# Seventy-four weight blocks of an encoder layer whose high part comes by a rounding transfer and whose low part is finished by an adding one

## The chip, the cores and the metric

The kernel runs on one core of one Trainium2 chip, in a single launch. The metric is the device time of one execution in microseconds. Its median before the change is 818.35 us over three runs, which lie between 818.23 and 818.53 us.

In the text TensorE appears in profile rows as PE (its weight loads as PEld), VectorE as DVE, ScalarE as ACT, GpSimd as POOL, and SyncE, which only issues transfers here, as SP.

## The reference, cut to what matters

One layer of a bidirectional encoder on 512 rows of width 1024 in float32, with retention, a spatial gating unit and a gated MLP of width 2816 with a short convolution:

```python
h = rmsnorm(x, g_pre_mix)
proj = h @ w_in                                        # 1024 x 7168: q k v g u sv a_ret a_sgu
y_ret = (layernorm(retention(q, k, v)) * silu(g)) @ w_ret_o
y_sgu = (gelu(u) * spatial(layernorm(gelu(sv)))) @ w_sgu_o
merged = sigmoid(a_ret) * y_ret + sigmoid(a_sgu) * y_sgu
x = x + rmsnorm(merged @ w_out, g_post_mix)
h2 = rmsnorm(x, g_pre_ffn)
hid = conv3(h2 @ w_up) + conv_b                        # 1024 x 5632
a, b = split(hid, 2)
x = x + rmsnorm((gelu(a) * b) @ w_down, g_post_ffn)    # 2816 x 1024
```

Nearly all the work is in products with weights. Together the weights are 146 blocks of 128 partitions by 1024 float32 numbers, 512 KB each, and every block is used by all 512 rows.

## The kernel before, in words

**Products in two parts.** TensorE multiplies in a shorter float32 form (`F32R`). To keep accuracy, each operand is written as a high part (the number rounded to that form) and a low part (what the rounding left over, rounded in turn). A product is three matmuls added up in PSUM: high by high, high by low and low by high (`mm3`, L230 to L233; `t_group`, L543 to L545; `Pair.product`, L762; `products`, L1170; `add_whole`, L1186). For activations and weights alike the two parts come from `split` (L100): ScalarE copies the source into the high tile (L95), which rounds it, and VectorE subtracts that from the source into the low tile (L102).

**Weight units.** The 146 blocks of `wall` lie in HBM in the order in which they are used. Some are taken whole, others are first combined into sums, so that fewer products are needed (a Strassen-like scheme). A list of units, written out by hand at the start, says in which order they are prepared:

- `blk` is one whole block (`w_block`, L145). It takes two slots of the weight ring, one for the high and one for the low part.
- `B11`, `B21`, `T1`, `T2`, `T3`, `T4`, `B22` are half-size forms made from a pair of blocks (`w_form`, L167); T1 and T3 are sums made on VectorE, T2 and T4 on GpSimd from the gates on (L181, L184). Each takes one slot, which holds both parts.
- `q` and `t` are the down projection's quarter forms (`w_down`, L192). Each takes two slots.

The **weight ring** has nine slots (`slot`, L142; the tag `w4`). It is handed out in turn: a unit gets the slot that nine slots earlier belonged to another unit, and may be written only when TensorE's last matmul that reads the earlier content has ended. The unit is prepared ahead of its use: `w_get` (L217) walks the list, as far ahead as the ring has room.

In the kernel before, every block comes over SP's queue into a **raw tile** of its own, of which there are four. `w_block` starts that load as soon as a raw tile is free, and then has `split` write the two slots. So what has to happen between a slot coming free and TensorE reading it is one ScalarE copy and one VectorE subtraction; the raw block is there already.

**The stages**, in order of time: q and k (whole blocks 0 to 7, to about 190 us with the retention's own work beginning); V, SV and g (whole blocks 8 to 31, four to a `t_group`, to about 414 us with retention between); u (forms alone); the gates (blocks 40 to 71, eight `gated_pair`s of one form pair and two whole blocks each); the output projection (blocks 72 to 79, of which 74 to 79 are kept in resident tiles of another pool); the up projection (blocks 80 to 123), whose hidden tiles are paired into eight **couples** (`Pair.part1`, `f_block`, `part2`, `f_block` with `part3` in its middle) except for tiles 0 to 3, 20 and 21, which use whole blocks; the down projection (blocks 124 to 145, nine `q`/`t` pairs and two whole blocks in each half) and the final norm.

In a pair of gates and in a couple, the units are prepared in the order B11, B21, T1, T2, whole block, T3, T4, B22, whole block. TensorE uses them in nearly this order: four products with B11, B21, T1 and T2, a complete `f_block` with the first whole block, a product with T3, half an `f_block` with the second whole block, products with T4 and B22, and the other half.

**What sets the order.** Each engine carries out its instructions in the order in which they stand in its own list. A scheduling layer arranges them from the program's order; `behind()` (L284) holds whole blocks behind the first two. An engine that waits for a semaphore keeps everything behind it waiting; this goes for the queue on which GpSimd issues transfers too, since the issues stand among its ordinary instructions. Before the change GpSimd has some T2 and T4 sums, small sums of the gates and norms, and a few loads and stores of activations.

Of the kernel before, what the change touches and what calls it, by code (L numbers as in the profile page):

```python
# [12 lines left out]
AF = mybir.ActivationFunctionType  # L13
ALU = mybir.AluOpType
# [5 lines left out]
KD = D // P  # L20
# [12 lines left out]
DOWN0 = NW - NF  # L33
# [3 lines left out]
UP0 = DOWN0 - 2 * NF  # L37
EARLY = 4
# [9 lines left out]
def tile_block(ctx: ExitStack, tc, xT, x, wall, par, cs, wsp, bsp, gpost, gffn, out):  # L48
    nc = tc.nc
# [6 lines left out]
    def nm(s):  # L56
        uid[0] += 1
        return f"{s}_{uid[0]}"

    def blk(dt=F32, n="blk", shape=(P, S)):  # L60
        return sb.tile(list(shape), dt, tag="blk", bufs=NBLK, name=nm(n))
# [35 lines left out]
    def as32(t):  # L97
        return t.bitcast(F32)

    def split(hi, lo, src):  # L100
        copy(hi, src)
        nc.vector.tensor_sub(lo, src, as32(hi))  # L102
# [3 lines left out]
    RES1 = NW - 22 - 44  # L106
    RES0 = RES1 - RES_OUT
    FORMS = ("B11", "B21", "T1", "T2", "T3", "T4", "B22")
    units = []
    i = 0  # L110
    while i < NW:
# [7 lines left out]
        elif i == UP0 + 2 * COUPLES[0][0]:  # L119
# [3 lines left out]
            i = UP0 + 2 * COUPLES[-1][1] + 2  # L123
# [12 lines left out]
    def raw_tile():  # L136
        return sb.tile([P, 1024], F32, tag="raw", bufs=4, name=nm("raw"))


    AT_64, AT_192 = 16, 48  # L140

    def slot(n, at=0, w=1024):  # L142
        return sb.tile([P, 1088], F32R, tag="w4", bufs=9, name=nm(n))[:, at : at + w]

    def w_block(i):  # L145
        raw = raw01[i] if i < 2 else raw_tile()
        resident = RES0 <= i < RES1
        if i > 1:
            nc.sync.dma_start(raw, wall[i])
        if resident:  # L150
            hi, lo = [], []
            for c in range(2):
                h_, l_ = blk(F32R, "wh"), blk(F32R, "wl")
                split(h_, l_, raw[:, c * S : (c + 1) * S])
                hi.append(h_)
                lo.append(l_)
        else:
            at = AT_192 if i >= DOWN0 else AT_64 if UP0 <= i < UP0 + EARLY else 0
            hi, lo = slot("wh", at), slot("wl", at)
            if i < 2:  # L160
                first_blocks(i, hi, lo, raw)
            else:
                with behind():
                    split(hi, lo, raw)
        return hi, lo
# [45 lines left out]
    def w_unit(u):  # L211
        return w_block(u[1]) if u[0] == "blk" else (w_down if u[0] in "qt" else w_form)(*u)
# [71 lines left out]
    def behind():  # L284

        both = ExitStack()
        for ins in lasts:
            both.enter_context(tc.issue_after(ins))
        return both

    def first_blocks(i, hi, lo, raw):

        last = {}

        def w_high(f, eng=copy):
            return eng(hi[:, f], raw[:, f])

        def w_low(f):
            return nc.vector.tensor_sub(lo[:, f], raw[:, f], as32(hi[:, f]))

        a, b, c = PIECES
        steps = (
            (x_high, 0, x01[0], T0), (w_high, a, nc.vector.tensor_copy), (w_high, b), (w_low, a), (w_low, b),
            (x_low, 0, x01[0], T0), (x_high, 0, x01[0], T1), (x_low, 0, x01[0], T1), (w_high, c), (w_low, c),
        ) if i == 0 else (
            (x_high, 1, x01[1], slice(0, S)), (x_low, 1, x01[1]),
            (w_high, HALVES[0]), (w_low, HALVES[0]), (w_high, HALVES[1]), (w_low, HALVES[1]),
        )
        for f, *args in steps:
            last[f] = tc.keep_in_program_order(f(*args))  # L310
        lasts[:] = last[w_high].ins, last[w_low].ins
# [75 lines left out]
    for t in range(NT):  # L387
        for n in range(2):
# [3 lines left out]
                out=xt, in_=xt, func=AF.Square, accum_out=ss[:, 4 * n + t : 4 * n + t + 1]  # L392
# [20 lines left out]
    for c in range(19, 1, -2):  # L413
        v.scalar_tensor_tensor(
            out=lc, in0=lc, scalar=1.0 / c, in1=lb, op0=ALU.add, op1=ALU.mult
        )
    v.scalar_tensor_tensor(out=lc, in0=lc, scalar=1.0, in1=la, op0=ALU.add, op1=ALU.mult)
    with behind():
        v.tensor_scalar(out=lg, in0=lgt, scalar1=0.0, scalar2=None, op0=ALU.min)
    v.scalar_tensor_tensor(  # L420
        out=lg, in0=lc, scalar=-2.0, in1=lg, op0=ALU.mult, op1=ALU.add
# [707 lines left out]
    i = 0  # L1129
# [335 lines left out]
```

## Time and profile before

| what | before |
|---|---|
| median of three runs | 818.35 us (818.23 to 818.53) |
| span of the profiled execution | 817.4 us |
| PE busy | 809.1 us, 99% |
| DVE busy | 659.9 us, 81% |
| ACT busy | 441.3 us, 54% |
| POOL busy | 86.0 us, 11% |
| moved by SP's queue | 86.76 MB |
| moved by GpSimd's queue | 4.46 MB |

The profile is one execution recorded by the hardware profiler. Its rows give a group of equal instructions by line, engine, output and inputs, shapes and count, then the busy time, the mean length of one in ns, and the idle time of that engine just before them with what ended it. Matmuls are pipelined: the length of one row is longer than the distance to the next, so the pace is read from start to start. The view of windows gives, for a stretch of time, each engine's busy time, the granted TensorE clock (1.00 is full) and the share of the 16 transfer engines in use. The view of transfers gives the time from issue to landing. The chain of waits is followed back from the last instruction of the program.

### The profile page before, as it was taken

The numbers are of one execution on the slowest core, as the hardware profiler recorded it, in microseconds if no ns is written. First come the engines' busy times: TensorE is split into PE (matmuls) and PEld (weight loads), VectorE is DVE, ScalarE is ACT, GpSimd is POOL, SyncE is SP. The second block draws the span as 40 slices with busy tenths as digits, with TensorE's granted clock in tenths as the row PEclk, the third lists the DMA queues.
The fourth block names the chain that finished last, engine by engine and source line by source line (L and its number), as shares of the span: only waits on it lengthen the run. The fifth ranks groups of instructions, "written<-read, shape, count | busy, mean of one in ns | idle before, by whom it ended". The sixth has DMA issues, their size and how long they took to land. (4 is left out here: it accounts for less than half of the span.)

```text
span 817.4 us, 13292 instructions
## 1 busy us (share of the span) xinstructions
PE 809.1 (99%) x5163; PEld 730.4 (89%) x5163; DVE 659.9 (81%) x1115; ACT 441.3 (54%) x777; POOL 86.0 (11%) x93
## 2 busy tenths in 40 slices
PE   9999999999999999999999999999999999999996
PEld 7888888888999999999988898899999898999996
DVE  7479897877898777767765659989999989987877
ACT  6546445536675444444445577556666666544441
POOL 0010000110001111132210210110111200000001
PEclk9999999999999999999999999999999999999998
DMA  8733222221333332233349111333333341233244
GB/s 287 259 117 103 78 79 77 77 79 65 103 103 105 104 103 90 91 103 103 107 165 335 53 51 66 104 103 104 104 103 103 103 156 52 77 130 110 97 155 155
DMA packets 29647, 93.24 MB, mean 114 GB/s; under 512 B 3536, under 2 KB 4432, under 8 KB 29584
## 3 DMA queue, kind: packets, MB, share of 16 engines
q1 hardware_dynamic: 27360, 86.76, 31.5%
q0 software_dynamic: 1360, 4.46, 1.6%
q10 hardware_dynamic: 864, 1.18, 0.4%
q8 instruction: 40, 0.66, 0.3%
q14 instruction: 23, 0.19, 0.1%
HBM read 88.19 MB, written 4.19 MB: 113 GB/s over the span
## 5 line engine op out<-in xcount | busy, mean ns | idle before, releaser
L102 DVE TENSOR_TENSOR wl<-raw,wh 128x1024 fp32r<-128x1024 f32 (+1 forms) x92 | 108.5, 1187 | 42.5 <-PE ps L762 20.0
L95 ACT ACTIVATE wf<-raw 128x512 fp32r<-128x512 f32 x140 | 85.0, 626 | 99.3 <-PE ps L232 34.0
L102 DVE TENSOR_TENSOR wf<-raw,wf 128x512 fp32r<-128x512 f32 x140 | 106.5, 773 | 25.3 <-ACT wf L95 24.5
L762 PE MATMUL ps<-sh,wf 128*128 128x256 f32 x640 | 118.8, 277 | 0.2 <-ACT c L95 0.2
L95 ACT ACTIVATE wh<-raw 128x1024 fp32r<-128x1024 f32 (+2 forms) x96 | 93.3, 983 | 39.2 <-PE ps L545 15.8
L762 PEld LDWEIGHTS ps<-sh,wf 128*128 128x128 f32 x640 | 100.9, 188 | 1.0 <-ACT c L95 0.4
L232 PE MATMUL ps<-h2l,wh 128*128 128x512 f32 (+1 forms) x256 | 92.5, 363 | 0.0
L231 PE MATMUL ps<-h2h,wh 128*128 128x512 f32 (+1 forms) x256 | 92.4, 364 | 0.0
L233 PE MATMUL ps<-h2h,wl 128*128 128x512 f32 (+1 forms) x256 | 92.3, 361 | 0.0
L762 PE MATMUL ps<-sl,wf 128*128 128x256 f32 x320 | 88.5, 277 | 0.0
L543 PE MATMUL ps<-wh,xh 128*128 128x512 f32 x192 | 75.0, 391 | 0.0
L544 PE MATMUL ps<-wl,xh 128*128 128x512 f32 x192 | 74.8, 390 | 0.0
L545 PE MATMUL ps<-wh,xl 128*128 128x512 f32 x192 | 74.7, 389 | 0.0
L762 PEld LDWEIGHTS ps<-sl,wf 128*128 128x128 f32 x320 | 60.1, 188 | 0.6
L1170 PE MATMUL ps<-dl,fh 128*128 128x256 f32 x216 | 59.8, 277 | 0.0
L1170 PE MATMUL ps<-dh,fh 128*128 128x256 f32 x216 | 59.7, 277 | 0.0
L1170 PE MATMUL ps<-dh,fl 128*128 128x256 f32 x216 | 59.7, 277 | 0.0
L233 PEld LDWEIGHTS ps<-h2h,wl 128*128 128x128 f32 x256 | 48.0, 188 | 7.7
L231 PEld LDWEIGHTS ps<-h2h,wh 128*128 128x128 f32 x256 | 47.8, 188 | 7.2 <-ACT h2h L994 0.3
L232 PEld LDWEIGHTS ps<-h2l,wh 128*128 128x128 f32 x256 | 48.1, 188 | 6.6
L762 PE MATMUL ps<-xh,wf 128*128 128x256 f32 x288 | 53.9, 278 | 0.0
L95 ACT ACTIVATE dh<-raw 128x768 fp32r<-128x768 f32 (+1 forms) x36 | 33.6, 949 | 34.4 <-DVE raw L204 18.9
(314 smaller groups left out, 2037.4 us busy)
## 6 DMA issues: line engine op xcount, KB each, us to landing
raw<-wall SPq DMA_DIRECT2D x144, 512.0 KB, 3.6
x<-x SPq DMA_DIRECT2D x24, 256.0 KB, 6.2
x<-x POOLq DMA_DIRECT2D x8, 256.0 KB, 2.4
xT<-xT SPq DMA_DIRECT2D x7, 256.0 KB, 4.7
xT<-xT POOLq DMA_DIRECT2D x4, 256.0 KB, 3.3
out<-zg SPq DMA_DIRECT2D x4, 256.0 KB, 2.0
raw<-wall SPq DMA_DIRECT2D x3, 256.0 KB, 4.7
out<-zs ACTq DMA_DIRECT2D x3, 256.0 KB, 2.4
```

Of the source, the lines that this page charges most:

```text
L95: return nc.scalar.activation(out=o, in_=i, func=AF.Copy)
L102: nc.vector.tensor_sub(lo, src, as32(hi))
L231: nc.tensor.matmul(o, ah, bh, start=start, stop=False, skip_group_check=skip)
L232: nc.tensor.matmul(o, ah, bl, start=False, stop=False, skip_group_check=skip)
L233: nc.tensor.matmul(o, al, bh, start=False, stop=stop, skip_group_check=skip)
L543: nc.tensor.matmul(acc[t], xh[k][:, c], wh[:, f], start=k == 0, stop=False)
L544: nc.tensor.matmul(acc[t], xh[k][:, c], wl[:, f], start=False, stop=False)
L545: part_end[0] = nc.tensor.matmul(acc[t], xl[k][:, c], wh[:, f], start=False, stop=k == KD - 1)
L762: self.last = nc.tensor.matmul(o, w_[:, c], a_, start=first and k == n == 0, stop=k == 3 and n == 2, skip_group_check=True,)
L1170: nc.tensor.matmul(o, a_[:, c], w_[:, f], start=j == t == i == 0, stop=j == DP - 1 and i == 2 and n not in (M2, M3, M4), skip_group_check= ...
```

## The change

For every whole block from the ninth on (`i >= KD`, with `KD` = 8) that is not one of the six resident ones, the raw tile, the load over SP's queue and the `split` are left out. In their place a new helper `w_added` gives the block two slots and does three things:

1. a transfer issued by GpSimd brings the block from HBM straight into the high slot, and converts float32 into the short form on the way;
2. ScalarE writes the negative of the high part into the low slot (an activation with scale −1);
3. a second transfer issued by GpSimd reads the same block from HBM again and adds it onto what stands in the low slot, so that raw minus high is left there.

These are 74 blocks: 24 of V, SV and g, 16 of the gates, 2 of the output projection, 28 of the up projection and 4 of the down projection. VectorE loses 74 subtractions of 128 x 1024, SP loses 74 loads, GpSimd gains 148 transfers, ScalarE has 74 copies as before, with another source. The order of TensorE's matmuls stays as it was, but for 27 in the last rows. Forms, `q` and `t` units, the first eight blocks and the resident ones are made as before.

```diff
@@ -142,9 +142,19 @@
     def slot(n, at=0, w=1024):
         return sb.tile([P, 1088], F32R, tag="w4", bufs=9, name=nm(n))[:, at : at + w]
 
+    def w_added(i, at):
+
+        hi, lo = slot("ah", at), slot("al", at)
+        nc.gpsimd.dma_start(hi, wall[i])
+        nc.scalar.activation(out=lo, in_=as32(hi), func=AF.Copy, scale=-1.0)
+        nc.gpsimd.dma_start(lo, wall[i], accum_op=ALU.add)
+        return hi, lo
+
     def w_block(i):
+        resident = RES0 <= i < RES1
+        if i >= KD and not resident:
+            return w_added(i, AT_192 if i >= DOWN0 else AT_64 if UP0 <= i < UP0 + EARLY else 0)
         raw = raw01[i] if i < 2 else raw_tile()
-        resident = RES0 <= i < RES1
         if i > 1:
             nc.sync.dma_start(raw, wall[i])
         if resident:
```

Line numbers of the changed kernel are ten higher from `w_block` on (its matmuls of `mm3` are L241 to L243, for instance); the three new operations are L148, L149 and L150.

## The prediction

> **What bounds the kernel now.** I read the busy table and the slices first, then what PE waits for, then the queues.
>
> ```profile
> span 817.4 us, 13292 instructions
> PE 809.1 (99%) x5163; PEld 730.4 (89%) x5163; DVE 659.9 (81%) x1115; ACT 441.3 (54%) x777; POOL 86.0 (11%) x93
> PE   9999999999999999999999999999999999999996
> q1 hardware_dynamic: 27360, 86.76, 31.5%
> q0 software_dynamic: 1360, 4.46, 1.6%
> ```
> ```profile
> PE ps L324 <- PEq L1455: 0.8, 1, 0.8
> PE ps L762 <- ACT c L95: 0.2, 1, 0.2
> ```
>
> (Queues: packets, MB, share of the span; waits: us, times, longest.) The second fence is the whole list of PE's waits: 1.0 us. TensorE sets the time; everything else matters only where it becomes late for TensorE. The profiled execution, 817.4 us, stands 0.95 below the median of 818.35; I add that at the end. Differences under 0.2% (1.6 us) cannot be told from none here.
>
> So the question is not what the change frees but whether the new way of making a weight block fits between the moment its slot in the ring of nine comes free and the moment TensorE needs it. Today a raw block is loaded ahead into one of four other tiles, and after the slot is free only two operations remain:
>
> ```profile
> L102 DVE TENSOR_TENSOR wl<-raw,wh 128x1024 fp32r<-128x1024 f32 x80 | 101.0, 1263 | 40.9 <-PE ps L762 20.0 <-issue 7.0 <-ACT wh L95 5.8
> L95 ACT ACTIVATE wh<-raw 128x1024 fp32r<-128x1024 f32 x80 | 84.5, 1057 | 35.3 <-PE ps L545 15.8 <-DMA raw<-wall 10.9 <-PE ps L762 4.7
> ```
>
> That is 1.06 + 1.26 = 2.3 us. Afterwards the rounding transfer writes the slot itself, so it cannot start earlier than the slot is free; the chain becomes transfer, ScalarE's negative, adding transfer.
>
> **The time it has.** TensorE's timeline in one coupled pair of the up stage:
>
> ```profile
> 536.31 0.28 PE L762 MATMUL ps<-h2h,wf 128*128 128x256 f32 x1
> ...
> 541.76 0.40 PE L231 MATMUL ps<-h2h,wh 128*128 128x512 f32 x1
> ...
> 547.23 0.28 PE L762 MATMUL ps<-sh,wf 128*128 128x256 f32 x1
> ...
> 548.60 0.40 PE L231 MATMUL ps<-h2h,wh 128*128 128x512 f32 x1
> ...
> 549.06 0.39 PE L233 MATMUL ps<-h2h,wl 128*128 128x512 f32 x1
> ...
> 556.81 0.28 PE L762 MATMUL ps<-h2h,wf 128*128 128x256 f32 x1
> ...
> 567.73 0.28 PE L762 MATMUL ps<-sh,wf 128*128 128x256 f32 x1
> ```
> ```profile
> 670.86 1.37 PE ps L762 x12
> ...
> 726.92 9.52 PE ps L1170 x84
> ```
>
> Units are taken in the order B11, B21, T1, T2, block, T3, T4, B22, block. Nine slots back from the second block's high part is B11's slot, its low part takes B21's. B11's product begins at 536.31 and takes 1.37 (twelve matmuls), so the slot is free at 537.7; the second block's high part is first read at 548.60, the low part at 549.06: 11.4 us. Taking 0.2 for the pipeline's drain and 0.2 for the weight load leaves 11.0. At 556.81 the next couple begins. The pairs of gate and up differ little, so this holds for 15 blocks: eight up couples and seven gate pairs. The first block of each pair, counted the same way, has 14 to 16 us. In the down stage two of the four whole blocks have between them and the slot's last reader a q, a t, a q and a t product, 84 matmuls: 9.5, so 9.3; the last two have two products of 1.37 between them less, 8.1, so 7.9. One block near 494 us has its high slot early but only 6.9 for negative and adding. The 24 blocks of the V, SV and g stage have 22 us and more, the rest above 12.
>
> **What the chain takes.** The landing times at hand:
>
> ```profile
> raw<-wall SPq DMA_DIRECT2D x144, 512.0 KB, 3.6
> ...
> xT<-xT POOLq DMA_DIRECT2D x4, 256.0 KB, 3.3
> ...
> gpf<-gffn POOLq DMA_DIRECT2D x2, 256.0 KB, 4.2
> ```
> ```profile
> raw<-wall SPq DMA_DIRECT2D x34, 512.0 KB, 4.1
> ```
> ```profile
> raw<-wall SPq DMA_DIRECT2D x11, 512.0 KB, 4.9
> ```
>
> The second fence is 240 to 410 us, the third 410 to 440, where the slices are full. q1 moved 86.76 MB in 31.5% of 817.4 us, 257 us: 337 GB/s, so 512 KB is 1.55 us of work and 256 KB 0.78.
>
> Rounding transfer: no row shows a Pool-queue transfer of 512 KB. Bounds: 3.6 (SP's) and 5.0 (4.2 + 0.78). Nearest is 3.3 + 0.78 = 4.1; I take 4.3, as more transfers will share the engines.
>
> Adding transfer: no row shows one at all. It must fetch the block and the negative already in the slot, and write the sum. From below a plain copy, 4.1; nothing excludes two copies end to end, 8.2. Reading a second 512 KB at q1's rate gives 4.1 + 1.5 = 5.6; with 0.6 for sharing (the landings above rise by 0.5 to 1.3 where more is moved) I take 6.2. [...]
>
> Handovers between engines, from the chain of waits:
>
> ```profile
> 631.84 0.61 DVE raw L178
> 632.67 1.66 POOL raw L181
> 634.35 0.63 ACT wf L95
> ```
>
> 0.22 from DVE's end to POOL's start, 0.02 from POOL to ACT: I take four of about 0.1. Chain: 4.3 + 1.06 + 6.2 + 0.45 = 12.0.
>
> **The sum.** What is late is the chain less the time it has:
> - 15 second blocks: 12.0 − 11.0 = 1.0 each, 15.
> - Two down blocks: 12.0 − 9.3 = 2.7 each, 5.4.
> - Last two down blocks: 12.0 − 7.9 = 4.1 once; the second lands behind the first while TensorE works on that.
> - Block near 494: 0.1 + 1.06 + 0.15 + 6.2 + 0.1 = 7.6 against 6.9, 0.7.
> - 24 early and some 30 other blocks: hidden by 12 to 22 us of matmuls. At chains above 14 the first blocks of the pairs are late too.
>
> Together 25. What is removed: 74 subtractions, 74 × 1.263 = 93 us of DVE, and 74 SP loads; the loads were done ahead and cost nothing. DVE is close to full in the couples:
>
> ```profile
> 557.00:578.50 21.50, 21.50 (x143) 19.56 (x143) 20.52 (x34) 13.85 (x26) 2.94 (x2) 1.00 0.32 102
> 727.00:736.00 9.00, 9.00 (x82) 9.00 (x81) 6.35 (x10) 3.78 (x4) 0.00 (x0) 1.00 0.18 59
> 811.00:817.00 6.00, 0.00 (x0) 0.00 (x0) 2.92 (x7) 0.18 (x2) 0.99 (x1) 0.60 0.47 175
> ```
>
> (columns: stretch, its length, busy us of PE, PEld, DVE, ACT, POOL, granted clock, DMA share, GB/s). DVE has 20.5 of 21.5, yet TensorE is busy all through, so relief is worth at most the waits listed, and I count nothing beyond 0.5. ScalarE's copies stay 74; the negative reads the slot instead of the raw tile, same shape, so 1.06. New is ScalarE's wait for the rounding transfer: behind it, in order, stand the rounding of the next form and a PSUM copy. In the next couple the slot is free at 556.81 + 1.37 = 558.2, the negative would end near 558.2 + 4.3 + 1.06 + 0.2 = 563.8, and the copy behind it near 564.2; the product at 567.73 is the first that needs the PSUM tile it empties. Covered by 3.5 us.
>
> Queues: Pool gains 148 transfers. An issue there takes it about 0.55 us,
>
> ```profile
> 188.58 0.55 POOL L817 DMA_DIRECT2D bst<-bsp  x1
> ```
> ```profile
> L181 POOL TENSOR_TENSOR raw<-raw,raw 128x512 f32<-128x512 f32 x15 | 26.4, 1762 | 240.1 <-DVE raw L178 171.0 <-ACT wf L95 62.2 <-DMA raw<-wall 6.9
> ```
>
> so 148 × 0.55 = 81 us beside 86 busy: it holds. But it is in order: a rounding transfer waits there for the slot, the adding one for ScalarE, and between them stand the T2 and T4 sums. T2's 1.76 can stand ahead of the rounding transfer of a first block: 14.0 − 0.2 − 1.8 = 12.0, which just covers the chain. It costs nothing at my prices and 15 × the excess above them. SP loses 74 loads and only gains room. DMA: in the couples the share is 0.32 at 102 GB/s; two blocks per 20.5 us (536.31 to 556.81), each with one or two more 512 KB readings, bring it to 0.5 or 0.65: not a bound.
>
> 817.4 + 25 + 0.95 = 843.4, less the 0.5: **843**.
>
> **Rivals.**
> *B, the adding transfer is as quick as a copy.* Chain 4.1 + 1.06 + 4.1 + 0.35 = 9.6: only the down blocks are late, 0.3 × 2 + 1.7 = 2.3: 820.7 (819 to 824). For it: transfers leave the engines two thirds idle, so much of a landing is fixed delay. Against: the second reading.
>
> *C, the adding transfer takes two copies end to end or more.* With 8.0 to 8.6 the chain is 13.8 to 14.4: 15 × 2.8 to 3.4 (42 to 51), down 9 to 10, last two 6, the block near 494 2.5 to 3, a few first blocks up to 10: 59 to 81, so 877 to 899. For it: read, then add into the same place, has two latencies. Against: pieces of one transfer overlap on 16 engines.
>
> [...]
>
> *D, Pool or ScalarE in order hold others back,* by 2 us in each of 16 pairs: 32 more than A, 875. Against: the 3.5 us of cover above.
>
> *E, faster.* If TensorE's pace suffers from DVE's traffic, or its waits go, DVE's 93 us less would show: decisive only if the chain takes under 7.9 us, because then nothing is late. Then the 1.0 us of waits goes and a little pace comes: 816. Against: that leaves the adding transfer 7.9 − 4.3 − 1.06 − 0.45 = 2.1 us, and TensorE's pace hardly minds DVE: a matmul of 256 columns takes 1.37 / 12 = 0.114 where DVE is 95% busy and 9.52 / 84 = 0.113 where it is 71% busy (727 to 736).
>
> *The change doesn't do what it says:* if the transfer left the bits unrounded, the low part would be zero and every time above the same.
>
> **How the numbers follow.** A, late second blocks at a moderate price, has 0.46 (its own range 828 to 862, low parts of 5.2 to 7.5 us); B 0.17; C 0.22; C2 0.07; D 0.04; E 0.04. The predicted time is A's. The range reaches from B's value to the top of C, 820 to 900, which leaves out E, C2 and the lower third of B: 0.17. Of B a third ends within 0.2% (below 820): same 0.06; faster 0.04 from E; slower the rest.
>
> **What would show it.** Landing of the rounding transfers near 4.3 and of the adding ones near 6.2 us; PE's waits no longer 1.0 but about 25 us, on the low part of the second whole block of each gate pair and couple (lines 241 to 243, about 1 us each), 2 to 4 us each at the four down blocks (1180); the V, SV and g stage without a wait; DVE busy near 567; ScalarE unchanged near 441. I am wrong if the adding transfers land under 4.5 or above 8, if waits show in the first 330 us, or if the waits are on the high part, which would mean that Pool issues late.

## The result, and the profile after

The changed kernel takes 860.61 us (median of four runs, 858.10 to 862.86) against 818.44 us: a ratio of 1.0513, 95% interval 1.0487 to 1.0538. It is 42 us slower. The profiled execution has a span of 856.9 us, 39.5 more than the one of before. The page's head and queues, where the columns of the queues are packets, MB and share of the span, and then the whole list of PE's waits (us, times, longest):

```profile
span 856.9 us, 13388 instructions
PE 819.3 (96%) x5163; PEld 732.6 (86%) x5163; DVE 580.9 (68%) x1041; ACT 437.2 (51%) x777; POOL 197.8 (23%) x241
q0 software_dynamic: 22672, 82.06, 42.0%
q1 hardware_dynamic: 16704, 47.96, 15.5%
```
```profile
PE ps L243 <- DMA al<-wall: 17.7, 13, 3.7
PE ps L1196 <- DMA al<-wall: 7.0, 3, 2.9
PE ps L772 <- ACT c L95: 2.3, 2, 1.2
PE ps L772 <- ACT sig L95: 1.9, 2, 1.7
PE ps L334 <- PEq L1465: 0.8, 1, 0.8
```

VectorE is 79 us less busy, and it buys nothing. TensorE, which had waited 1.0 us in all, now waits 29.7 us, 24.7 of them for an adding transfer to land in a low slot. Its own busy time has grown as well, by 10 us, although its instructions are the same: in two stretches, shown below, it ran at about half the clock (0.52 and 0.54), and it loses some 0.1 us more behind each wait.

The subtractions of whole blocks fell as forecast, from 101.0 us (80 rows) to 7.3 (6 rows). VectorE is still busy 580.9 us and not 567: rows overlap a little, and some others grew (the eight of L822 from 0.80 to 1.25 us at the mean).

The view of transfers gives the prices that the profile of before did not have:

```profile
ah<-wall POOLq DMA_DIRECT2D x74, 512.0 KB, 4.1
al<-wall POOLq DMA_DIRECT2D x74, 512.0 KB, 5.8
raw<-wall SPq DMA_DIRECT2D x70, 512.0 KB, 4.5
```

I set each matmul's start against the start of the same matmul before; their order is the same up to the last rows. Where the difference jumps, TensorE waited; where it creeps, TensorE ran slower. A jump comes out 0.2 to 0.5 us longer than the wait in the profile's row, as it holds what TensorE loses at its restart as well. The split between the two depends a little on where a jump is taken to end. Up to 250 us there is neither. Then:

| stretch (times of before) | jumps | creep |
|---|---|---|
| gates, 250 to 425 | 13.3 | 3.6 |
| start of up, 500 to 525 | 0.5 | 0.1 |
| couples, 525 to 675 | 10.8 | 1.2 |
| down, 700 to 800 | 7.5 | 2.0 |

Together 39.0; the first matmuls came 0.5 earlier and 0.3 crept elsewhere, so that the last one is 38.8 us late.

The gates stand at 250 to 425 us. The list of stages ahead of the prediction, in which V, SV and g last to about 414 us, has this wrong: in the trace of before, the last matmul of that stage (L545) starts at 211.9 us.

Two views show the gates' most expensive wait and what followed it. TensorE's timeline, with the idle time before a row and what ended it, and the windows behind it (length, busy us of PE, PEld, DVE, ACT, POOL, granted clock, DMA share, GB/s):

```profile
425.81 0.40 PE L242 MATMUL ps<-yl,ah 128*128 128x512 f32 x1
429.87 0.80 PE L243 MATMUL ps<-yh,al 128*128 128x512 f32 x1 [3.67 <-DMA al<-wall]
430.46 0.63 PE L241 MATMUL ps<-yh,ah 128*128 128x512 f32 x1
```
```profile
424.00:430.00 6.00, 2.25 (x15) 1.82 (x15) 0.42 (x1) 1.47 (x3) 2.88 (x4) 0.92 1.02 240
430.00:436.00 6.00, 6.00 (x19) 5.03 (x20) 0.00 (x0) 1.06 (x1) 0.60 (x1) 0.52 0.73 225
```

After the wait of 3.7 us (a jump of 4.2) the granted clock was 0.52 for some 6 us, and that cost another 2.6. GpSimd's timeline says why this wait is longer than in other pairs:

```profile
410.35 0.88 POOL L150 DMA_DIRECT2D al<-wall  x1 [5.40 <-ACT al L149]
411.42 1.66 POOL L904 TENSOR_TENSOR sig<-sig,r 128x512 f32<-128x512 f32 x1 [0.18 <-DVE sig L903]
415.14 1.67 POOL L904 TENSOR_TENSOR sig<-sig,r 128x512 f32<-128x512 f32 x1 [2.07 <-DVE sig L903]
416.76 0.59 POOL L148 DMA_DIRECT2D ah<-wall  x1
```

The slot of this block was free at 414.4 us. Its rounding transfer was issued at 416.8, because two of the gates' own sums (L904) stand ahead of it in GpSimd's list and the second waited for VectorE until 415.1.

### The profile page after: what moved, and what is told of

Its sections match the earlier page's. It is cut to its first block, busy times and chain, and to the rows that moved or that the text cites. A ratio compares the mean times of both kernels' runs of the same rounds, so it can differ in the third digit from the quotient of the medians.

```text
span 856.9 us, 13388 instructions
## 1 busy us (share of the span) xinstructions
PE 819.3 (96%) x5163; PEld 732.6 (86%) x5163; DVE 580.9 (68%) x1041; ACT 437.2 (51%) x777; POOL 197.8 (23%) x241
## 4 chain that ended last, share of the span: by engine, by line
PE 60%; DMA 15%; issue 13%; DVE 5%; POOL 4%; ACT 3%; POOLq 0%; DVEq 0%; ACTq 0%
PE ps L772 9%; DMA al<-wall 7%; PE ps L243 7%; PE ps L1180 7%; DMA ah<-wall 7%; PE ps L242 7%; PE ps L241 7%; PE ps L553 5%; PE ps L554 5%; PE ps L555 5%; POOL raw L191 2%; PE ps L936 2%; PE ps L935 2%; PE ps L934 2%; DVE wf L102 1%
## 5 line engine op out<-in xcount | busy, mean ns | idle before, releaser
L149 ACT ACTIVATE al<-ah 128x1024 fp32r<-128x1024 f32 x74 | 78.5, 1060 | 167.0 <-DMA ah<-wall 93.3
L148 POOL DMA_DIRECT2D ah<-wall x74 | 44.0, 599 | 299.2 <-PE ps L772 83.7
L150 POOL DMA_DIRECT2D al<-wall x74 | 65.0, 878 | 188.9 <-ACT al L149 152.2
L243 PE MATMUL ps<-h2h,al 128*128 128x512 f32 (+1 forms) x256 | 93.4, 366 | 7.7 <-DMA al<-wall 7.7
L242 PE MATMUL ps<-h2l,ah 128*128 128x512 f32 (+1 forms) x256 | 92.6, 363 | 0.0
L241 PE MATMUL ps<-h2h,ah 128*128 128x512 f32 (+1 forms) x256 | 92.5, 364 | 0.0
L553 PE MATMUL ps<-ah,xh 128*128 128x512 f32 x192 | 75.0, 391 | 0.0
L554 PE MATMUL ps<-al,xh 128*128 128x512 f32 x192 | 74.8, 390 | 0.0
L555 PE MATMUL ps<-ah,xl 128*128 128x512 f32 x192 | 74.7, 389 | 0.0
L243 PEld LDWEIGHTS ps<-h2h,al 128*128 128x128 f32 x256 | 48.0, 188 | 19.2 <-DMA al<-wall 11.8
L242 PEld LDWEIGHTS ps<-h2l,ah 128*128 128x128 f32 x256 | 48.1, 188 | 6.7
L241 PEld LDWEIGHTS ps<-h2h,ah 128*128 128x128 f32 x256 | 47.9, 188 | 6.8 <-ACT h2h L1004 0.3
```

The source lines that it names most:

```text
L149: nc.scalar.activation(out=lo, in_=as32(hi), func=AF.Copy, scale=-1.0)
L150: nc.gpsimd.dma_start(lo, wall[i], accum_op=ALU.add)
L241: nc.tensor.matmul(o, ah, bh, start=start, stop=False, skip_group_check=skip)
L242: nc.tensor.matmul(o, ah, bl, start=False, stop=False, skip_group_check=skip)
L243: nc.tensor.matmul(o, al, bh, start=False, stop=stop, skip_group_check=skip)
L553: nc.tensor.matmul(acc[t], xh[k][:, c], wh[:, f], start=k == 0, stop=False)
```

## The experiments

Two theories stand at the start. The first: the chain of rounding transfer, negative and adding transfer is longer than the time between free slot and use. The second: the sums that GpSimd has to make hold up the transfers behind them in its own order, and what hangs on those. They ask for different cures.

**The sums moved away from GpSimd** (`sums_dve`). The chain is untouched.

```diff
-            eng = nc.vector if i < GATE0 or i == UP0 + 2 * COUPLES[0][0] else nc.gpsimd
+            eng = nc.vector
...
-            eng = nc.vector if i < GATE0 else nc.gpsimd
+            eng = nc.vector
...
-            nc.gpsimd.tensor_tensor(out=t, in0=t, in1=r[2 * j + i], op=ALU.add)
+            v.tensor_tensor(out=t, in0=t, in1=r[2 * j + i], op=ALU.add)
```

> The T2 and T4 sums and the gates' 8 sums move from GpSimd to VectorE, so that GpSimd has almost only transfers to issue. Theory 1 (only the chain of transfer, negative and adding transfer is too long for its slot): nothing but the order on GpSimd changes, the 29.7 us of PE's waits stay within 2 us and the time is about 860. Theory 2 (GpSimd, in order, issues the rounding transfers of the last three second blocks of the gates 2.4 to 2.8 us after their slot is free, because two sums stand ahead of them): PE's waits of 2.46, 1.93 and 4.20 us in the gates fall to 0.5 or less, the granted clock does not fall at 430 us (2.6 us), PE's waits on the copies c (2.3) become shorter since T2 is done earlier: about 848.

Measured: 848.18 us, ratio 1.0365 (1.0331 to 1.0400). The two largest of PE's waits are left, and none for ScalarE:

```profile
PE ps L243 <- DMA al<-wall: 13.7, 11, 2.3
PE ps L1196 <- DMA al<-wall: 6.2, 3, 3.0
```

The three last waits in the gates fell, as jumps, from 2.46, 1.93 and 4.20 us to 1.05, 0.89 and 2.47 (0.5 or less was expected), the clock did not fall behind the last (it was 1.00 over 425 to 445 us), and the waits on c and sig are gone. So the sums on GpSimd cost 12.4 us of the 42 (9.6 between the two profiled executions; the four runs of each kernel spread over 5 to 6 us). The run takes the sums out of the transfers' way and makes them shorter at once: T2's mean is 1.96 us on GpSimd, on VectorE it takes 0.68. The two effects are not told apart. The rest of the loss remains with GpSimd free of sums.

**The blocks with little time made as before** (`not_tight`). Now the chain is removed where it was late, and the sums stay on GpSimd.

```diff
+    def tight(i):
+        return i >= DOWN0 or (GATE0 <= i < GATE1 and (i - GATE0) % 4 == 3) or (i - UP0) in [2 * b + 1 for _, b in COUPLES]
...
-        if i >= KD and not resident:
+        if i >= KD and not resident and not tight(i):
```

> The second whole block of each gate pair and couple and the four down blocks (20 of 74) are made as before, by load, copy and subtraction; the other 54 keep the two transfers. Theory 1 (only blocks with less than about 12 us between free slot and use are late): 818.4 to 821. Rival (148 transfers on GpSimd's queue and 38 MB more read slow things everywhere): 54/74 of the loss of 42 us stays, about 849.

Measured: 831.46 us, ratio 1.0155 (1.0140 to 1.0170); neither 818 to 821 nor 849. PE's list of waits has no adding transfer:

```profile
PE ps L775 <- ACT c L95: 4.8, 4, 1.8
PE ps L937 <- DVE sig L906: 3.2, 2, 2.2
PE ps L775 <- ACT sig L95: 1.8, 1, 1.8
```

My expectation was wrong here: I had taken the sums on GpSimd to matter only where a late rounding transfer makes a low part late. ScalarE's list shows the other way, here for the longest wait on c (GpSimd, then ScalarE, then TensorE; T2 is L194 here, and L775 is the product that waits for c):

```profile
623.63 2.44 POOL L194 TENSOR_TENSOR raw<-raw,raw 128x512 f32<-128x512 f32 x1 [14.87 <-DVE raw L191]
626.02 0.59 POOL L148 DMA_DIRECT2D ah<-wall  x1
629.82 1.06 ACT L149 ACTIVATE al<-ah 128x1024 fp32r<-128x1024 f32 x1 [1.96 <-DMA ah<-wall]
634.90 0.37 ACT L95 ACTIVATE c<-ps 128x256 f32<-128x256 f32 x1
635.32 0.38 PE L775 MATMUL ps<-sh,wf 128*128 128x256 f32 x1 [1.81 <-ACT c L95]
```

The rounding transfer of a first block, which has time enough itself, stands behind T2. ScalarE waits for it with the negative, and from there to the copy c it works without a break, so c comes late with it. The waits on sig at 431 and 435 us stand behind a negative too, whose transfer stood behind another block's adding one in GpSimd's list. These 12.8 us and the 29.5 that `sums_dve` keeps make 42.3, the whole of the loss: in size the two causes add up. The waits are not the same ones, though: those on c and sig are 9.8 us here and 4.2 in the changed kernel, where TensorE is later.

**Both cures** (`both`: the two diffs together; 54 blocks still come by transfers).

> The two cures at once: the 20 blocks with little time made as before, the other 54 by transfers, and the T2, T4 and gate sums on VectorE. If the loss of 42 us has two independent causes (chain too long for its slot, 29 us, and work that GpSimd's order holds up, 13 us), nothing is left: 818.4 to 819.5. If something else is behind it (traffic, more waits of TensorE on other units), some 3 us or more stay. If VectorE's 54 subtractions less count for something, under 817.5.

Measured: 820.63 us, ratio 1.0027 (1.0018 to 1.0036). Of the 42 us 2 are left, a little over the 819.5 expected. The view of PE's waits shows where some of them are (beside the 0.8 for PEq that the kernel before has too):

```profile
PE ps L938 <- DMA al<-wall: 0.5, 1, 0.5
PE ps L246 <- DMA al<-wall: 0.4, 1, 0.4
PE ps L938 <- DVE wl L102: 0.2, 1, 0.2
```

They are at 430 to 440 us, in the output projection, and at 496 us, at the block for which the prediction had a short time. The profiled execution was 1.1 us over that of before; the runs spread from 818.71 to 822.63, and what makes some of them longer than the profiled one stays open.

**Only the blocks with much time** (`first24`).

```diff
-        if i >= KD and not resident:
+        if KD <= i < U0:
```

> Only the 24 blocks of the V, SV and g stage are made by transfers. Theory 1 (17 us and more are enough): no wait of PE in the first 250 us and 818.4 within 0.8. Relief theory (VectorE's time counts): 24 subtractions of 1.26 us less on VectorE, up to 1 us faster. Traffic rival: 24/74 of 42 us, 832.

Measured: 818.51 us, ratio 0.9999 (0.9990 to 1.0008). PE's waits are 1.3 us, nearly those of before. VectorE's busy time falls to 634.9 us, 25 less, and no time is won; 24 blocks' more transfers cost nothing either.

**Only the gates' sums moved** (`gate_sums`: the last line of `sums_dve` alone).

> The changed kernel (860.6) with only the gates' eight sums on VectorE; T2 and T4 stay on GpSimd. The theory that these eight hold up the rounding transfers of the last three second blocks of the gates: the waits of 2.46, 1.93 and 4.20 us fall to about 1.0, 0.9 and 2.5 (as with all sums moved), the clock stays up at 430 us (2.6), the waits on ScalarE's copies c and sig (4.2) stay: about 853. If T2 and T4 are what counts: 860.

Measured: 857.71 us, ratio 1.0474 (1.0458 to 1.0489); I had expected 853. PE's list:

```profile
PE ps L243 <- DMA al<-wall: 17.9, 15, 2.2
PE ps L1196 <- DMA al<-wall: 6.4, 3, 3.0
PE ps L772 <- ACT c L95: 2.2, 2, 1.1
PE ps L772 <- ACT sig L95: 1.7, 1, 1.7
```

The mechanism is in part as expected: the three waits are 1.03, 0.83 and 2.41 us, and the waits on c and sig stay. But the total on L243 did not shrink, because other second blocks, in the gates at 293 and 316 us and in the couples, were later than in the changed kernel by up to 1.0 us each. The eight sums explain those three waits; of the 12.4 us they bring 2.9, and the other 9.5 come only when T2 and T4 are moved too.

**An adding transfer that doesn't add** (`plain_lo`; the low parts are then no remainders, so the addition is left out of the computation).

```diff
-        nc.gpsimd.dma_start(lo, wall[i], accum_op=ALU.add)
+        nc.gpsimd.dma_start(lo, wall[i])
```

> The second transfer overwrites the low slot with the rounded block and adds nothing (the low parts are then no remainders: the addition is left out). Theory 1 (the adding transfer's second reading makes the chain late): its landing falls from 5.8 to about 4.1 us, the chain from 12.0 to about 10.4; the couples' waits of 0.8 to 1.6 vanish (8.5 us together), the down blocks' fall from 2.4, 2.0 and 3.1 to about 0.7, 0.4 and 1.4, the gates' by 1.7 each, and the clock stays up: about 836. Rival (a transfer on GpSimd's queue that waits for ScalarE lands late whether it adds or not): landing stays at 5.8, time at 860.

Measured: 840.39 us, ratio 1.0261 (1.0237 to 1.0285). The landing and PE's list:

```profile
al<-wall POOLq DMA_DIRECT2D x74, 512.0 KB, 4.1
```
```profile
PE ps L772 <- ACT c L95: 5.1, 4, 2.4
PE ps L772 <- ACT sig L95: 5.0, 2, 3.3
PE ps L1196 <- DMA al<-wall: 2.8, 3, 1.3
PE ps L243 <- DMA al<-wall: 1.8, 4, 1.1
```

The price of adding is 5.8 − 4.1 = 1.7 us, and with it go 20 of the 24.7 us of waits on `al`. The waits on ScalarE, 10.1 us here against 4.2, took part of the gain back, as in `not_tight`, and the time is 4 us over the 836 expected: where TensorE no longer waits for the low part, it comes earlier to what stands in ScalarE's list behind a negative or behind the copy of T2.

**Only the four down blocks** (`down4`).

```diff
-        if i >= KD and not resident:
+        if i >= DOWN0:
```

> Only the four whole down blocks by transfers. Chain theory: waits of 2.4, 2.0 and 3.1 us as in the changed kernel, 7.5, and nothing else: 826. With the clock falling after the first of them, as at 753 us there (1.7 us): 827.6. Were the down waits a consequence of the lateness before, 818.4.

Measured: 831.09 us, ratio 1.0151 (1.0135 to 1.0166). Four blocks of 146 cost 12.5 us. PE waits three times for `al`, 7.8 us in all, near the 7.5 expected, so these waits are no consequence of lateness before. The time is 3.5 us over the 827.6 expected at most: on top of the waits the profiled execution lost 2.8 us in creep, since the clock fell after two of the waits (it was 0.83 over 720 to 730 us and again over 740 to 750, and 1.00 in the other stretches of 10 us up to 810) and not after one. Its span, 828.7 us, is 2.4 under the median, where that of before is 1.0 under its own; so the timed executions lost somewhat more than the profiled one.

**The adding transfer in two halves** (`halves`, on top of `sums_dve`).

```diff
-        nc.gpsimd.dma_start(lo, wall[i], accum_op=ALU.add)
+        for f in (slice(0, S), slice(S, 2 * S)):
+            nc.gpsimd.dma_start(lo[:, f], wall[i, :, f], accum_op=ALU.add)
```

> The kernel with the sums on VectorE (848.2), its adding transfer split into two of 512 columns, 256 KB each. TensorE reads the first half of the low part first, 2.7 us ahead of the second. If a landing is a fixed part and a part by bytes, the first half lands after about 4.3 us for 5.8, the chain to the first low read is 1.5 shorter, and most waits of 0.9 to 2 us vanish: about 835. If the cost is fixed per transfer, or the queue serves the halves by turns so that both land at 6, nothing changes: 848, or a little above with 74 more issues on GpSimd.

Measured: 857.52 us, ratio 1.0478 (1.0461 to 1.0496), against 848.18 without it. The first half lands 4.5 us after its issue (median; 4.3 was expected), and the waits of the second blocks (L244 in this kernel) are 8.8 us instead of 13.7. But the second lands 6.6 us after the first one's issue, and in the down stage, where `add_whole` reads it three matmuls later, TensorE waits twice:

```profile
741.67 0.36 PE L1197 MATMUL ps<-al,fh 128*128 128x256 f32 x1 [2.40 <-DMA al<-wall]
741.86 0.28 PE L1197 MATMUL ps<-ah,fl 128*128 128x256 f32 x1
741.98 0.28 PE L1197 MATMUL ps<-ah,fh 128*128 128x256 f32 x1
744.82 0.58 PE L1197 MATMUL ps<-al,fh 128*128 128x256 f32 x1 [2.56 <-DMA al<-wall]
```
```profile
740.00:744.00 4.00, 0.59 (x3) 0.42 (x3) 2.01 (x3) 1.52 (x2) 0.00 (x0) 1.00 0.95 215
744.00:752.00 8.00, 7.18 (x37) 7.18 (x38) 2.32 (x4) 0.00 (x0) 0.00 (x0) 0.57 0.23 77
```

The waits of the down blocks are 11.1 us instead of 6.2, and creep is 11.5 instead of 6.8.

**The negative on VectorE** (`neg_dve`, on top of `sums_dve`).

```diff
-        nc.scalar.activation(out=lo, in_=as32(hi), func=AF.Copy, scale=-1.0)
+        nc.vector.tensor_scalar_mul(lo, as32(hi), -1.0)
```

> The kernel with the sums on VectorE (848.2), the negative made by VectorE and not by ScalarE. Chain theory: a shorter step (1.06 us on ScalarE; VectorE's may take 0.6 to 1.1) takes up to 0.45 off each late block: 840 to 848. Rival: VectorE, the busier of the two, waits in its own order for the rounding transfer and holds evacuations and subtractions behind it: 850 to 865. [...]

Measured: 861.74 us, ratio 1.0530 (1.0481 to 1.0579), 13.6 us above `sums_dve`. The groups of this kernel, by form:

```profile
L149 DVE TENSOR_SCALAR al<-ah 128x1024 fp32r<-128x1024 f32 x74 | 51.1, 691 | 97.6 <-DMA ah<-wall 52.4 <-PE ps L772 40.7 <-PE ps L554 2.9
```

The step itself is shorter, 0.69 for 1.06 us, and the kernel slower: VectorE now stands idle 97.6 us before its negatives, with its other work behind them. TensorE's added waits are all on adding transfers, 32.0 us against 19.9:

```profile
PE ps L243 <- DMA al<-wall: 21.3, 16, 5.2
PE ps L1196 <- DMA al<-wall: 10.7, 3, 4.6
```

In the second blocks of the couples the chain from issue to landing is no shorter, 11.9 us at the mean as in `sums_dve`: what the negative saves goes into the handovers behind it, 0.7 us for 0.4. Why more blocks are late was not followed further. The issues of the adding transfers took 0.87 us at the median, as in `sums_dve` and the changed kernel (0.87 and 0.88): the negative's move did not lengthen them.

**Ten slots** (`ring10_sums`, `ring10_sums_nodown`, `r10b`, all on top of `sums_dve`). The first has this diff, the second also makes the down blocks as before, the third leaves the look-ahead (last line) at nine.

```diff
-        return sb.tile([P, 1024], F32, tag="raw", bufs=4, name=nm("raw"))
+        return sb.tile([P, 1024], F32, tag="raw", bufs=3, name=nm("raw"))
...
-        return sb.tile([P, 1088], F32R, tag="w4", bufs=9, name=nm(n))[:, at : at + w]
+        return sb.tile([P, 1088], F32R, tag="w4", bufs=10, name=nm(n))[:, at : at + w]
...
-n + w_size(units[w_pos[1]]) <= max(room, 9 if look == LOOK else 0)
+n + w_size(units[w_pos[1]]) <= max(room, 10 if look == LOOK else 0)
```

> The kernel with the sums on VectorE (848.2) gets ten weight slots for nine, and three raw tiles for four. A second block's rounding transfer may start one product earlier, 1.37 us (gates: up to 3.2). Chain theory: of the 13.7 us of waits on adding transfers in gates and couples under 3 stay, the 6.2 of the down blocks stay since their time between slot and use is the same 9.5: about 834. Rival (the landing time is set by ScalarE's or GpSimd's order and not by when the slot comes free): no change, 848. Three raw tiles could make the loads of the forms late; that would show as waits of ScalarE or VectorE on raw<-wall.

> The same, with the four whole down blocks made as before. Chain theory: another 6.2 us of waits and about 1.7 of clock less than ring10_sums, 820 to 826. Rival (lateness adds up and is only moved): as ring10_sums.

> The kernel with the sums on VectorE (848.2) with ten weight slots for nine and three raw tiles for four, but the look-ahead left at nine slots (in ring10_sums it was ten, and ScalarE's negatives came to stand ahead of the retention's work in its list). Chain theory: the second blocks' transfers start one product earlier, the waits on adding transfers in gates and couples fall from 13.7 to under 4, the down blocks' 6.2 stay; no waits in the first 240 us: about 838. If three raw tiles were what made ring10_sums slow, the waits of 30 us in the first 240 us come back: 870 and more.

Measured: 885.77, 875.65 and 884.31 us, ratios 1.0805, 1.0686 and 1.0809. As a cure it fails; my expectations missed by 46 to 52 us. As a test of the couples it speaks: waits of 8.8 us on adding transfers there with nine slots (`sums_dve`) became 1.4 in `r10b`, since the transfers start a product earlier. The time went elsewhere, much of it into the first 240 us. ScalarE's waits of `r10b`, and the same row of `sums_dve` behind it:

```profile
ACT al L149 <- DMA ah<-wall: 197.2, 66, 10.3
```
```profile
ACT al L149 <- DMA ah<-wall: 86.3, 32, 12.6
```

With a slot free earlier the scheduling layer put negatives earlier into ScalarE's list, ahead of the retention's evacuations, and there ScalarE waited for the rounding transfers to land while TensorE waited for the evacuations behind them (7.4 us in `r10b` for the values' low part vl alone). The look-ahead isn't the reason, since `r10b` is as slow as `ring10_sums`. By its number alone `r10b` came out as I had written for the rival, the three raw tiles (870 and more, with the lost time in the first 240 us). ScalarE's waits speak against it: in the first 260 us it waits 90.3 us for rounding transfers (7.7 in `sums_dve`) and 7.1 for raw loads. How much is due to the three raw tiles was still not separated; nine slots with three raw tiles were not run.

No version beat the kernel before. `first24` equals it.

## Why the prediction was right, and where it was not

The time lies in the stated range, at 42 us of loss where 25 were forecast. That it does is owed in part to the width of the range, which was stretched to 900 for slower adding transfers; these did not come. Two terms that the sum has at nothing make up the 17 us between: the sums on GpSimd (12.4) and TensorE's slower pace behind its waits (6.8). The late chains themselves came to 22.8, two less than forecast.

*The bound and the place were right.* TensorE sets the time, and what counts is the time between a slot coming free and its use. All the waits on adding transfers stand on the low part (L243, L1196) and after 250 us; the 24 early blocks cost nothing. One sign of being wrong did come: TensorE waits in the first 330 us, at 254, 269 and 292 us, 3.9 us in all. The sign seems meant for the stage of V, SV and g, which has no wait; but that stage ends at 212 us, and these are waits of the gates.

*The prices were right.* Rounding 4.1 us at the median (taken 4.3), negative 1.06, adding 5.8 (taken 6.2, and 5.6 before the term for sharing). The trace agrees with the 5.6 in size: adding costs 1.7 us more than the same transfer without it (`plain_lo`), where one more reading was priced at 1.5. That the reading costs this, and not the sum, no run here separates, and a landing does not double: 4.1 against 5.8. An issue takes GpSimd 0.60 us at the mean for a rounding transfer and 0.88 for an adding one, 109 us in all and not the 81 of the prediction. The handovers on the way were larger than taken, 0.3 to 0.4 us from the free slot to the issue and from the negative to the next issue. From the trace's single blocks, the chain in the second blocks of the couples was 11.3 to 12.7 us (taken 12.0), in the down blocks 11.2 to 11.9.

*The terms.* Taken: 15 second blocks at 1.0. Measured: seven couples wait 0.81 to 1.56, 8.5 together, one does not wait at all. Taken for the down blocks 5.4 and 4.1; measured 4.4 and 3.1. For the block near 494 us 0.7 was taken; in the changed kernel TensorE does not wait for it. A block 11 us further on, which has no term, costs 0.5. In the gates the term was wrong: four of the seven are on time within 0.4 us, as their chain is 11.1 to 11.5, and the three last lose 8.6 us. One more, the first pair's second block, which the prediction had among "the rest above 12", lost 2.2: its rounding transfer was issued 0.6 us after another block's adding transfer and took 8.4 us to land. That the gates' second blocks come to 8.6 us where seven times 1.0 was taken is luck: four chains are shorter than taken, and of the 8.6 about half comes from the sums on GpSimd (4.4 are left in `sums_dve`).

*The step that failed* is "it costs nothing at my prices", on GpSimd's order, and with it the 0.04 for rival D. I had named T2 and T4 as what stands between the transfers, and left out the gates' sums (L904), which the last pairs have; and I looked only for what delays transfers, not for what they delay. The chain of waits of before, which I quoted for its handovers alone, already showed a path from T1 over T2 on GpSimd, its copy on ScalarE and further steps to a copy c, for which TensorE waits 0.2 us, that is a path with no slack. In the changed kernel, VectorE's timeline (T1), GpSimd's and then TensorE's have:

```profile
631.55 0.68 DVE L188 TENSOR_TENSOR raw<-raw 128x512 f32<-128x512 f32 x1
632.38 2.80 POOL L191 TENSOR_TENSOR raw<-raw,raw 128x512 f32<-128x512 f32 x1 [4.55 <-issue]
635.13 0.59 POOL L148 DMA_DIRECT2D ah<-wall  x1
```
```profile
636.17 0.39 PE L772 MATMUL ps<-h2h,wf 128*128 128x256 f32 x1 [1.24 <-ACT c L95]
```

T2 took 2.80 us, 1.66 in the quoted row of before, and TensorE waited 1.24 for the copy c, which stands in ScalarE's list behind the copy of T2. No transfer held this T2: GpSimd had stood idle for 4.55 us and began when T1 was done. It was late by its own length; what stretched it is not known (the mean of all 15 is 1.96, and 1.76 before). The rounding transfer behind it went out 2.8 us after T2's start; in `sums_dve` the same one goes out 2.9 us before it (at 624.24, T2 at 627.17). "Covered by 3.5 us" was worked out for the negative of a second block. It did not cover the copy behind T2, nor the copies behind the negative of a first block: in the changed kernel such a one (sig, at 254 us) costs 1.7, and its rounding transfer stood behind a T4 sum. The sums on GpSimd cost 12.4 us by `sums_dve` and 12.8 by `not_tight`.

*The clock* has 0.07 of the chances, as rival C2, and there only on top of slow adding transfers; the prediction's row of 811 to 817 us has 0.60 with TensorE idle throughout, and how short a wait brings a fall, and what one costs, no run had shown. It fell at the prices of A: creep is 7 us, 2.6 of it behind the wait of 3.7 us and 1.7 behind one of 2.2; most of the rest is the 0.1 us behind each wait, at full clock. So 25 us became 42: 22.8 of jumps and 6.8 of creep with the sums off GpSimd (`sums_dve`), and 12.4 by those sums.

*Relief for VectorE* was taken as 0.5 at most. 25 us less (`first24`) and 54 less (`both`) changed nothing for the better.

## What to carry to other kernels

When a preparation is moved from a load ahead of time into the slot itself, add up the whole chain from the slot's release and set it against the time for each kind of use; the shortest ones decide, and four blocks of 146 can cost 12 us. Moving transfers to the queue of an engine that also computes had a second effect here: transfers waited behind that engine's sums (one went out 2.4 us after its slot was free), and a third engine that waited for a late transfer held up what stood behind it in its own list (1.8 us of TensorE's time at the longest on a copy c in `not_tight`). So every path that already runs without slack through one of these engines belongs in the sum. Relieving an engine that the bounding engine does not wait for was worth nothing here.

## What the runs showed of the hardware that was not expected

The granted clock fell behind some waits of 1.9 to 3.7 us and not behind others: it was 0.52 between 430 and 436 us, behind a wait of 3.7 us, 0.54 between 753 and 756 us, behind a wait of 2.2 us on an adding transfer, and 1.00 between 836 and 840 behind one of 2.9 (and up to 852 us). In `sums_dve` it was 0.83 over 740 to 750 us, a stretch in which TensorE is idle for 1.9.

```profile
753.00:756.00 3.00, 2.89 (x14) 2.89 (x15) 1.53 (x3) 0.00 (x0) 0.00 (x0) 0.54 0.21 85
836.00:840.00 4.00, 3.54 (x30) 3.54 (x31) 0.69 (x1) 0.00 (x0) 0.00 (x0) 1.00 0.58 112
```

What tells these cases apart is not known from these runs; the two falls in the changed kernel cost 1.7 and 2.6 us, some three quarters of the waits before them. The second surprise is that two adding transfers of half the size land 4.5 and 6.6 us after the first issue, where a single one lands after 5.7 or 5.8.
